# A hybrid backbone step: the RNN branch's gating behind its gates, two temporaries for Strassen's sums, modulation at every fourth product

## The chip, the cores and the metric

One core of one Trainium2 chip runs the whole kernel. The metric is the device time of one execution in microseconds (us); lower is better. The names in the profile: PE is TensorE (matmuls; PEld its weight loads), DVE VectorE, ACT ScalarE, POOL GpSimd, SP the queue that issues the DMAs.

## The reference

A step of two layers over two groups of tokens that share weights (128 context tokens and 1024 latent tokens, 1152 columns in the kernel). Each layer projects the modulated, normalised input into three mixers (a gated bidirectional RNN, latent attention, windowed attention) and their gates, merges them and adds the result to the residual. What the change touches is the RNN branch, whose product with its SiLU gate is formed in the merge, and the projection of the merge logits:

```python
    mod = jax.nn.silu(cond) @ p["w_mod"] + p["b_mod"]
    shift, scale, gate = jnp.split(mod, 3, axis=-1)
    h = rmsnorm(x, p["g_norm"]) * (1 + scale[:, None, :]) + shift[:, None, :]
    parts = jnp.split(h @ p["w_in"], _in_split_points(), axis=-1)
...
    r = jax.nn.sigmoid((jnp.einsum("blnc,ncd->blnd", xb, w_a).reshape(B, L, D_RNN) + b_a).astype(jnp.float32))
    i = jax.nn.sigmoid((jnp.einsum("blnc,ncd->blnd", xb, w_i).reshape(B, L, D_RNN) + b_i).astype(jnp.float32))
    log_a = LRU_C * r * jax.nn.log_sigmoid(lam.astype(jnp.float32))
    a = jnp.exp(log_a)
    u = jnp.sqrt(-jnp.expm1(2.0 * log_a)) * i * x.astype(jnp.float32)
...
    xc = centred_conv(x_rnn, p["conv_w"], p["conv_b"])
    h_f = rglru_scan(xc, h0_f, p["lru_wa"][0], p["lru_ba"][0], p["lru_wi"][0], p["lru_bi"][0], p["lru_lam"][0], False)
    h_b = rglru_scan(xc, h0_b, p["lru_wa"][1], p["lru_ba"][1], p["lru_wi"][1], p["lru_bi"][1], p["lru_lam"][1], True)
...
    m = jax.nn.sigmoid(merge_logits.astype(jnp.float32)).astype(y_rnn.dtype).reshape(B, L, N_BRANCH, D_MODEL)
    u = (m[:, :, 0] * ((y_rnn * jax.nn.silu(g_rnn)) @ p["w_br_rnn"])
```

## The kernel before

Activations lie with features on the partitions and the 1152 tokens along the free axis, cut into three chunks of 384 (CH). Every fp32 matmul is made of three reduced ones, on a high and a low half of each operand: a `split` casts the high half on ACT (L212) and subtracts for the low half on POOL or DVE (L218); the names end in h and l. A weight is loaded into a ring of three raw buffers (`wr`) and then split.

**The RNN stage** of a layer goes over eight feature tiles of 128 (ft 0 to 7). For each, `rnn_units` gives three units. The *x unit* (tile in, feature ft) has three pieces of 24 matmuls; `ev_x` copies each out of PSUM into `xpad` on ACT, and after the third DVE forms the convolution in `xc` (L563, then L566 three times), ACT casts `xh`, POOL subtracts `xl`. The *g unit* (also tile in, feature 8 + ft) has three such pieces; `ev_g` takes a sigmoid into `gsil` on ACT (L577) and multiplies on DVE (L578), which makes the SiLU. The *gates* are 12 pieces of three matmuls on xh and xl (tile g), each evicted by a sigmoid on ACT (L591) into r0, i0, r1 or i1, through three PSUM buffers. After the last gate `scan()` follows: tanh, exp and sqrt on ACT (L604 to L613), eight long elementwise operations and four scan instructions on DVE (L608 to L621), the sum of both directions (L624), two multiplications with gsil (L625, L626) and the store to `yr` (L627). `gsil`, `xc`, `xpad`, `xh` and `xl` are one buffer each.

PE's order is the order of the program (`manual_schedule`). `steps(ft)` takes 18 pieces of a tile, and after piece i as many *fillers* as the table RF has at i: pieces of other projections (tm with 384, 288 or 256 columns, and in), whose PSUM tile is another one; a filler in three is followed by a piece of a mod unit. So 18 pieces are, in order, x (3), g (3) and 12 gates; at tile 0 x and g stand interleaved (`both`). The fillers stand behind the third g piece (3), the fourth and the eighth gate (1 each) and the last gate (2). The evictions of the fillers go through two buffers `eo` (ocq, ock, oqs, okv, osl, osg) and DMAs. On ACT, DVE and POOL a scheduler sets the order by the readiness that it computes; each engine runs its queue strictly in that order.

**The Strassen stage** follows: `combine` forms sums of quadrants of the activations, T1, T2, T4 and a last one that overwrites B12, four elements each, with three DVE operations (L839 to L841), a cast on ACT and a subtraction on DVE. Each element uses one of the five slots of the tile `et` in rotation; slots 0, 1 and 2 are afterwards c1, xs and u2, into which the products are gathered. Then come 11 pairs of seven products (tile st, weights wsh and wsl); `evac` gathers the products (L903 to L918), and after every fifth product `mod_step` takes a piece of a mod unit. Layer 1 has no mod units.

Of the kernel before, what the change touches and what calls it, by code (L numbers as in the profile page):

```python
# [34 lines left out]
V_BMOD, V_G, V_CW, V_CB, V_BA, V_BI, V_LAM, V_H0, V_N = 0, 24, 32, 64, 72, 88, 104, 120, 136  # L35
R_QN, R_KN, R_SINK, R_N = 0, 384, 640, 648

RF = (0,) * 5 + (3, 0, 0, 0, 1, 0, 0, 0, 1, 0, 0, 0, 2)
M_SCORE = set("a0 a1 a2 b1 b2 b0 ra0 ra1 ma xa sa na rb0 rb1 mb xb sb nb c cr cx cs cn".split())
M_START = (  # L40
# [154 lines left out]
def _backbone(ctx, tc, nc, a, depth):  # L195
# [302 lines left out]
    for l in range(depth):  # L498
# [34 lines left out]
        with ExitStack() as rst:  # L533
# [17 lines left out]
            def rnn_units(ft):  # L551
# [21 lines left out]
                def ev_g(c, ps):  # L573
                    if c == 0:
                        r["gsil"] = rp.tile([P, T], F32, tag="gsil", name=f"gsil{l}_{ft}")
                    o = r["gsil"][:, c * CH:(c + 1) * CH]
                    nc.scalar.activation(out=o, in_=ps, func=ACT.Sigmoid)  # L577
                    nc.vector.tensor_tensor(out=o, in0=o, in1=ps, op=ALU.mult)  # L578

                def gate(d, g, c, w):  # L580
                    gh, gl = w
                    xh, xl = r["xh"], r["xl"]
                    if c == 0:
                        t = "ri"[g] + str(d)
                        r[t] = rp.tile([P, RW], F32, tag=t, name=f"{t}{l}_{ft}")
                    dst, vb = r["ri"[g] + str(d)], (V_BA, V_BI)[g]
                    c0, c1 = c * CH, (c + 1) * CH if c < 2 else RW
                    ps = psr.tile([P, 512], F32, tag="a", name=f"g{l}_{ft}_{d}{g}{c}")
                    j = 2 * d + g
                    mm3(ps[:, 0:c1 - c0], [((gh[:, j], gl[:, j]), (xh[:, c0:c1], xl[:, c0:c1]))])  # L590
                    nc.scalar.activation(out=dst[:, c0:c1], in_=ps[:, 0:c1 - c0], func=ACT.Sigmoid,  # L591
                                         bias=sv[:, vb + 8 * d + ft:vb + 8 * d + ft + 1])
                    if g == 1 and c == 2:
                        nc.gpsimd.tensor_tensor(out=dst, in0=dst, in1=r["xc"], op=ALU.mult)
                        if d == 1:
                            scan()

                def scan():
                    rr, ii = [r["r0"], r["r1"]], [r["i0"], r["i1"]]
                    tt = [f(rp.tile([P, RW], F32R, tag=t, name=f"t{t}{l}_{ft}")) for t in ("xh", "xl")]  # L600
                    gsil = r["gsil"]
                    for d in range(2):
                        j = 8 * d + ft
                        nc.scalar.activation(out=tt[d], in_=rr[d], func=ACT.Tanh, scale=L["s4"][:, j:j + 1])  # L604
                    for d in range(2):
                        j = 8 * d + ft
                        nc.scalar.activation(out=rr[d], in_=rr[d], func=ACT.Exp, scale=L["m8"][:, j:j + 1])
                        nc.vector.scalar_tensor_tensor(out=rr[d], in0=rr[d], scalar=1.0, in1=tt[d], op0=ALU.add, op1=ALU.mult)  # L608
                        nc.vector.scalar_tensor_tensor(out=rr[d], in0=rr[d], scalar=-2.0, in1=tt[d], op0=ALU.add, op1=ALU.mult)
                        nc.vector.scalar_tensor_tensor(out=tt[d], in0=rr[d], scalar=2.0, in1=rr[d], op0=ALU.add, op1=ALU.mult)  # L610
                        nc.gpsimd.tensor_scalar(out=rr[d], in0=rr[d], scalar1=1.0, scalar2=1.0, op0=ALU.mult, op1=ALU.add)
                    for d in range(2):
                        nc.scalar.activation(out=tt[d], in_=tt[d], func=ACT.Sqrt, scale=-1.0, bias=tiny_t[:, 0:1])  # L613
                    for d in range(2):
                        nc.vector.tensor_tensor(out=ii[d], in0=ii[d], in1=tt[d], op=ALU.mult)
                        for s0, s1, ctxp in ((0, NL, False), (CTX, CTX + P, True)):
                            av, uv, hv = rr[d][:, s0:s1], ii[d][:, s0:s1], tt[d][:, s0:s1]
                            if d == 1:
                                av, uv, hv = av[:, ::-1], uv[:, ::-1], hv[:, ::-1]
                            init = 0.0 if ctxp else sv[:, V_H0 + 8 * d + ft:V_H0 + 8 * d + ft + 1]  # L620
                            nc.vector.tensor_tensor_scan(out=hv, data0=av, data1=uv, initial=init, op0=ALU.mult, op1=ALU.add)  # L621
                    nc.gpsimd.tensor_copy(out=rg[:, l, 0, ft:ft + 1], in_=tt[0][:, CTX + P - 1:CTX + P])
                    nc.gpsimd.tensor_copy(out=rg[:, l, 1, ft:ft + 1], in_=tt[1][:, CTX:CTX + 1])
                    nc.vector.tensor_tensor(out=tt[0][:, 0:CTX + P], in0=tt[0][:, 0:CTX + P], in1=tt[1][:, 0:CTX + P], op=ALU.add)  # L624
                    nc.vector.tensor_tensor(out=gsil[:, 0:NL], in0=gsil[:, 0:NL], in1=tt[0][:, 0:NL], op=ALU.mult)  # L625
                    nc.vector.tensor_tensor(out=gsil[:, NL:T], in0=gsil[:, NL:T], in1=tt[0][:, CTX:CTX + P], op=ALU.mult)  # L626
                    nc.sync.dma_start(out=yr_d[ft], in_=gsil)  # L627
# [4 lines left out]
                    ins = [both(ins, ((0, 0), (0, 1), (1, 0), (1, 1), (0, 2), (1, 2)))]  # L632
                elif ft == 0:
                    ins = [(lambda: first, both(ins, [(i, c) for c in range(NCH) for i in range(2)])[1])]
                return ins + [
                        (lambda: wload(a["w_lru"][l, ft], 4, P, f"lru{l}_{ft}"), gates)]

            def both(us, order):
                return (lambda: [u[0]() for u in us]), [lambda w, i=i, c=c: us[i][1][c](w[i]) for i, c in order]
# [122 lines left out]
            def mod_step(n=3):  # L762
                count[0] += 1
                if count[0] % n == 0 and G:
                    next(G[0], None)

            def steps(ft):
                for i in range(18):
                    if ft == 0 and i == 4:
                        with tc.high_priority(offset=400):  # L770
                            late_norm()
                    next(R)
                    for _ in range(2 if ft == 0 and i == 5 else RF[i]):
                        filler()
                    yield

# [31 lines left out]
            with tc.manual_schedule(engines={mybir.EngineType.PE}):  # L808
# [25 lines left out]

                def combine(dst, a, b):
                    for k in range(4):
                        t = slot[nt[0] % 5]
                        nt[0] += 1
                        nc.vector.tensor_tensor(out=t, in0=f(a[0][k]), in1=f(b[0][k]), op=ALU.subtract)  # L839
                        nc.vector.tensor_tensor(out=t, in0=t, in1=f(a[1][k]), op=ALU.add)  # L840
                        nc.vector.tensor_tensor(out=t, in0=t, in1=f(b[1][k]), op=ALU.subtract)  # L841
                        split(dst[0][k], dst[1][k], t, "act", "dve")
# [24 lines left out]
                def pair(m):  # L867
# [22 lines left out]
                    def product(i, w):  # L890
                        b = (B11, T1, T2, B21, B12, B22, T4)[i]
                        for c0, c1_ in SP:
# [2 lines left out]
                                for z, (x, y) in enumerate(((0, 0), (0, 1), (1, 0))):  # L895
                                    nc.tensor.matmul(ps, w[x][:, k], b[y][k][:, c0:c1_], start=k == 0 and z == 0, stop=k == 3 and z == 2)  # L896
                            evac(i, ps, slice(c0, c1_))
                        mod_step(5)
                        if i == 6 and m + 2 == PAIRED:
                            ys_load()  # L900

# [1111 lines left out]
```

## Time and profile before

| | us |
|---|---|
| median of 3 runs | 3316.56 (3313.89 to 3320.11) |
| the profiled run | 3312.14 |
| its span | 3310.4 |
| PE busy | 3143.1 (95%) |
| POOL / DVE / ACT busy | 1695.9 / 2114.8 / 1608.7 |
| mean granted clock of PE | 0.978 |

The RNN stage runs from 116 to about 640 us in layer 0 and from 1762 to about 2260 us in layer 1, the Strassen stage directly behind it. The waits of PE are read by what released it: "PE g <- ACT r" is time in which the next gate matmul stood until ACT had evicted an r. A timeline row gives start, duration, engine, line, operation, out<-in, form, and in brackets how long the engine had been idle ahead of it and what released it. The granted clock is 1.00 at 2.4 GHz and 0.50 at 1.2 GHz.

### The profile page before, as it was taken

How to read it: one execution, taken by the hardware profiler on the slowest of the kernel's cores; microseconds unless marked ns; L12 is line 12 of the kernel's file. 1: busy time of each engine (PE TensorE's matmuls, PEld its weight loads, DVE VectorE, ACT ScalarE, POOL GpSimd, SP SyncE). 2: the span in 40 equal slices, each digit the busy share in tenths (PEclk: the TensorE clock that was granted, in tenths of full speed). 3: DMA queues.
4: the chain of work that ended last, by engine and by line, in shares of the span. 5: the costliest groups of instructions: out<-in, count | busy, mean ns of one | idle time of the engine just before them, and what ended most of it. 6: DMA issues, size and time to landing. Idle time of an engine off the chain costs nothing. (4 is left out here: it accounts for less than half of the span.)

```text
span 3310.4 us, 54421 instructions
## 1 busy us (share of the span) xinstructions
PE 3143.1 (95%) x20100; PEld 3006.4 (91%) x20100; DVE 2114.8 (64%) x3777; ACT 1608.7 (49%) x3191; POOL 1695.9 (51%) x1328
## 2 busy tenths in 40 slices
PE   7998989899999999999999999998999999999998
PEld 4998989899999999898989999998999999989998
DVE  5554655854344888977575446577344388898766
ACT  4444545333323777764344454543333277776532
POOL 3755656566622444455475456655553144445643
PEclk9999999999999999999999999999999999999999
DMA  5222122233362001456542221222225400045564
GB/s 211 88 89 83 60 89 93 83 109 124 119 210 95 23 25 45 121 163 208 168 150 74 77 69 47 69 75 90 103 99 191 139 21 27 25 109 150 188 202 133
DMA packets 240330, 351.21 MB, mean 106 GB/s; under 512 B 72512, under 2 KB 183232, under 8 KB 239808
## 3 DMA queue, kind: packets, MB, share of 16 engines
q1 hardware_dynamic: 240064, 347.73, 32.8%
q8 instruction: 159, 2.61, 0.3%
q14 instruction: 107, 0.88, 0.1%
HBM read 248.87 MB, written 98.78 MB: 105 GB/s over the span
## 5 line engine op out<-in xcount | busy, mean ns | idle before, releaser
L242 PE MATMUL in<-hh,wh_in 128*128 128x384 f32 x1248 | 428.1, 343 | 5.9 <-DVE osl L725 3.3
L242 PE MATMUL in<-hh,wl_in 128*128 128x384 f32 x1248 | 427.0, 342 | 6.6 <-POOL wl_in L218 6.6
L242 PE MATMUL in<-hl,wh_in 128*128 128x384 f32 x1248 | 428.2, 343 | 4.1 <-DVE hl L423 4.1
L903 DVE TENSOR_TENSOR et<-st,et 128x320 f32<-128x320 f32 (+1 forms) x352 | 152.1, 454 | 281.9 <-PE st L896 281.1
L1256 POOL TENSOR_SCALAR p<-p,mx 128x1152 f32<-128x1152 f32 x128 | 157.8, 1233 | 201.0 <-DVE mx L1253 125.0
L242 PEld LDWEIGHTS in<-hh,wh_in 128*128 128x128 f32 x1248 | 240.0, 192 | 8.8 <-DVE osl L725 4.8
L242 PEld LDWEIGHTS in<-hl,wh_in 128*128 128x128 f32 x1248 | 239.2, 192 | 8.1 <-DVE hl L423 7.9
L242 PEld LDWEIGHTS in<-hh,wl_in 128*128 128x128 f32 x1248 | 239.4, 192 | 7.6 <-POOL wl_in L218 7.6
L1307 DVE TENSOR_TENSOR pl<-pt,ph 128x512 fp32r<-128x512 f32 (+1 forms) x320 | 201.5, 637 | 28.1 <-ACT ph L1303 25.2
L896 PE MATMUL st<-hh,wsl 128*128 128x320 f32 (+1 forms) x704 | 208.4, 296 | 8.3 <-POOL wsl L218 8.3
L1303 ACT CAST ph<-pt 128x512 fp32r<-128x512 f32 (+1 forms) x320 | 170.8, 552 | 91.2 <-PE pt L1296 86.5
L242 PE MATMUL tm<-twh,hh 128*128 128x256 f32 (+2 forms) x720 | 214.4, 298 | 0.0
L242 PE MATMUL tm<-twl,hh 128*128 128x256 f32 (+2 forms) x720 | 213.7, 297 | 0.0
L242 PE MATMUL tm<-twh,hl 128*128 128x256 f32 (+2 forms) x720 | 213.7, 297 | 0.0
L218 POOL TENSOR_TENSOR wsl<-wr_in,wsh 128x512 fp32r<-128x512 f32 x88 | 147.7, 1678 | 122.5 <-ACT wsh L212 122.5
L896 PE MATMUL st<-hh,wsh 128*128 128x320 f32 (+1 forms) x704 | 208.6, 296 | 1.8 <-ACT osg L732 1.8
L896 PE MATMUL st<-hl,wsh 128*128 128x320 f32 (+1 forms) x704 | 208.0, 295 | 0.0
L1296 PE MATMUL pt<-ident,p 128*128 128x128 f32 x1152 | 171.1, 274 | 10.0 <-DVE kl L1166 4.3
L218 POOL TENSOR_TENSOR wl_in<-wr_in,wh_in 128x1024 fp32r<-128x1024 f32 x50 | 133.6, 2675 | 69.8 <-ACT wh_in L212 69.8
L1296 PEld LDWEIGHTS pt<-ident,p 128*128 128x128 f32 x1152 | 132.7, 140 | 34.6 <-DVE pl L1307 12.1
L1321 PE MATMUL o<-ph,v 128*128 128x256 f32 x576 | 153.1, 292 | 0.0
L1321 PE MATMUL o<-pl,v 128*128 128x256 f32 x576 | 145.9, 280 | 0.0
(498 smaller groups left out, 10619.5 us busy)
## 6 DMA issues: line engine op xcount, KB each, us to landing
wr_in<-in_w_fm SPq DMA_DIRECT2D x96, 512.0 KB, 3.4
sg<-et SPq DMA_DIRECT2D x88, 288.0 KB, 2.1
wr_wm<-in_w_mod SPq DMA_DIRECT2D x32, 512.0 KB, 3.4
wr_wo<-in_w_out SPq DMA_DIRECT2D x32, 512.0 KB, 3.6
yr<-gsil SPq DMA_DIRECT2D x16, 576.0 KB, 2.8
msgrnn<-sg SPq DMA_DIRECT2D x48, 192.0 KB, 2.4
u<-msgrnn SPq DMA_DIRECT2D x48, 192.0 KB, 2.5
qr<-qs SPq DMA_DIRECT2D x36, 256.0 KB, 4.3
```

The source lines that it names most:

```text
L218: eng.tensor_tensor(out=lo, in0=src, in1=f(hi), op=ALU.subtract)
L242: nc.tensor.matmul(ps, x, y, start=n == 0, stop=n == last)
L896: nc.tensor.matmul(ps, w[x][:, k], b[y][k][:, c0:c1_], start=k == 0 and z == 0, stop=k == 3 and z == 2)
L903: add = lambda o, y: nc.vector.tensor_tensor(out=o[:, cs], in0=ps, in1=y[:, cs], op=ALU.add)
L1256: nc.gpsimd.tensor_scalar(out=pts[i], in0=pts[i], scalar1=mxs[i][:, 5:6], scalar2=1.0, op0=ALU.mult, op1=ALU.mult)
L1296: nc.tensor.transpose(ps[:, w:w + P], pts[q][:, k * P:(k + 1) * P], ident)
L1303: nc.scalar.copy(out=r["h", j][:, 0:width(j)], in_=r["t", j][:, 0:width(j)])
L1307: nc.vector.tensor_tensor(out=r["l", j][:, 0:width(j)], in0=r["t", j][:, 0:width(j)], in1=f(r["h", j][:, 0:width(j)]), op=ALU.subtract)
L1321: nc.tensor.matmul(O[:, 0:256], V[k][:, h % 4, :], x[:, 256 * i:256 * i + 256], start=k == 0 and e == 0, stop=k == 8 and e == 1)
```

## The change

Three things are changed, as the diff shows. The new function `gated` holds the two multiplications with gsil and the store.

```diff
-RF = (0,) * 5 + (3, 0, 0, 0, 1, 0, 0, 0, 1, 0, 0, 0, 2)
+RF0 = (0,) * 5 + (3, 0, 0, 0, 1, 0, 0, 0, 1, 0, 0, 0, 2)
+RF = (0, 0, 3, 0, 0, 0, 0, 1, 0, 0, 0, 1, 0, 0, 0, 0, 0, 2)
...
                     nc.vector.tensor_tensor(out=o, in0=o, in1=ps, op=ALU.mult)
+                    if ft and c == 2:
+                        gated()
...
                         if d == 1:
                             scan()
+                            if ft == 0:
+                                gated()
...
-                    gsil = r["gsil"]
+                    r["t"] = tt
...
+
+                def gated():
+                    gsil, tt = r["gsil"], r["t"]
                     nc.vector.tensor_tensor(out=gsil[:, 0:NL], in0=gsil[:, 0:NL], in1=tt[0][:, 0:NL], op=ALU.mult)
                     nc.vector.tensor_tensor(out=gsil[:, NL:T], in0=gsil[:, NL:T], in1=tt[0][:, CTX:CTX + P], op=ALU.mult)
                     nc.sync.dma_start(out=yr_d[ft], in_=gsil)
...
-                return ins + [
-                        (lambda: wload(a["w_lru"][l, ft], 4, P, f"lru{l}_{ft}"), gates)]
+                ins.insert(1, (lambda: wload(a["w_lru"][l, ft], 4, P, f"lru{l}_{ft}"), gates))
+                return ins
...
-                    for _ in range(2 if ft == 0 and i == 5 else RF[i]):
+                    for _ in range((RF if ft else RF0)[i]):
...
-                        t = slot[nt[0] % 5]
+                        t = slot[2 + nt[0] % 2 * 2]
...
-                        mod_step(5)
+                        mod_step(4)
```

For tiles 1 to 7 the order of a tile is now x (3), gates (12), g (3); three fillers stand between x and the gates, one behind the fifth gate piece, one behind the ninth and two behind g. At tile 0 three fillers instead of two stand ahead of the gates. All matmuls stay; a filler that is taken earlier is missing at the end of the stage. `combine` uses slots 2 and 4 in turn.

The order of ACT's instructions from the convolved x of tile 3 to its first gate, before (twh, wh_wm and wh_in are weight casts, ock evictions of tm pieces):

```order
L212 CAST xh_3_2455<-xc_3_2450 128x1156
L577 ACT_TABLE_LOAD
L577 ACTIVATE gsil_3_2490<-in_11_0_2465 128x384
L577 ACTIVATE gsil_3_2490<-in_11_1_2493 128x384
L212 CAST wh_in_4_2661<-wr_in_4_2663 128x1024
L577 ACTIVATE gsil_3_2490<-in_11_2_2520 128x384
L664 ACTIVATE ock_6_2572,ssck_6_2573<-tm_1_6_2547 128x256
...
L212 CAST wh_wm_5_3_2651<-wr_wm_5_3_2653 128x1024
L591 ACTIVATE r_3_2667<-g_3_000_2668,sv_110 128x384
```

And now, from the last copy into xpad; the sigmoids of gsil 3 are no longer there:

```order
L562 COPY xpad_508<-in_3_2_2457 128x128
L672 ACTIVATE ock_7_2518,ssck_7_2519<-tm_1_7_2493 128x256
L686 COPY ock_7_2518<-tm_1_7_2493 128x32
L672 ACTIVATE ock_8_2552,ssck_8_2553<-tm_1_8_2527 128x256
L213 CAST twh_2_2573<-twr_2_0_2575 128x2x256
...
L213 CAST xh_3_2489<-xc_3_2484 128x1156
L213 CAST wh_wm_5_3_2563<-wr_wm_5_3_2565 128x1024
...
L732 ACT_TABLE_LOAD
L732 ACTIVATE osl<-in_21_0_2591 128x384
L213 CAST twh_2_2573<-twr_2_3_2587 128x2x256
L594 ACTIVATE r_3_2626<-g_3_000_2627,sv_110 128x384
```

The cast of xh and the evictions of the fillers have stayed; the first gate's eviction now has a sigmoid of a filler ahead of it, with a table load. Behind the gates of tile 2 stand now gsil 2's sigmoids, with a table load of their own, between exp (L612) and sqrt (L618):

```order
L612 ACT_TABLE_LOAD
L612 ACTIVATE r_2_2138<-r_2_2138,m_115 128x1156
L612 ACTIVATE r_2_2071<-r_2_2071,m_115 128x1156
L578 ACT_TABLE_LOAD
L578 ACTIVATE gsil_2_2261<-in_10_0_2236 128x384
L578 ACTIVATE gsil_2_2261<-in_10_1_2264 128x384
L213 CAST wh_lru_3_2399<-wr_lru_3_2401 128x512
L578 ACTIVATE gsil_2_2261<-in_10_2_2291 128x384
L618 ACT_TABLE_LOAD
L618 ACTIVATE txl_2_2206<-txl_2_2206,consts 128x1156
```

Before, a cast and evictions alone stood between the exponential (L607) and the load for the square root (L613); the two loads are now three.

On DVE the convolution of tile 3 (L563, L566) stood among the scan's last instructions before:

```order
L621 SCALAR_TENSOR_TENSOR txh_2_2259<-r_2_2114,sv_110,i_2_2130 128x1024
L621 SCALAR_TENSOR_TENSOR txh_2_2259<-r_2_2114,i_2_2130 128x128
L563 TENSOR_SCALAR xc_3_2450<-xpad_508,sv_110 128x1156
L566 SCALAR_TENSOR_TENSOR xc_3_2450<-xpad_508,sv_110,xc_3_2450 128x1156
L624 TENSOR_TENSOR txh_2_2259<-txh_2_2259,txl_2_2260 128x1155
L566 SCALAR_TENSOR_TENSOR xc_3_2450<-xpad_508,sv_110,xc_3_2450 128x1156
L625 TENSOR_TENSOR gsil_2_1937<-gsil_2_1937,txh_2_2259 128x1024
L626 TENSOR_TENSOR gsil_2_1937<-gsil_2_1937,txh_2_2259 128x128
L566 SCALAR_TENSOR_TENSOR xc_3_2450<-xpad_508,sv_110,xc_3_2450 128x1156
```

And now:

```order
L629 TENSOR_TENSOR txh_2_2205<-txh_2_2205,txl_2_2206 128x1155
L633 TENSOR_TENSOR gsil_2_2261<-gsil_2_2261,txh_2_2205 128x1024
L634 TENSOR_TENSOR gsil_2_2261<-gsil_2_2261,txh_2_2205 128x128
L564 TENSOR_SCALAR xc_3_2484<-xpad_508,sv_110 128x1156
L567 SCALAR_TENSOR_TENSOR xc_3_2484<-xpad_508,sv_110,xc_3_2484 128x1156 x2
```

The convolution now stands behind the gated product of the tile before.

## Rows read from the trace of the kernel before

**Rows 1.** the page's part 1, PE: busy time, share, instructions.

```profile
PE 3143.1 (95%) x20100; PEld 3006.4 (91%) x20100; DVE 2114.8 (64%) x3777; ACT 1608.7 (49%) x3191; POOL 1695.9 (51%) x1328
```

**Rows 2.** the waits of PE: engine, line, waited for: us in total, times, longest.

```profile
PE g L242 <- ACT r L591: 34.9, 8, 6.5
PE st L896 <- POOL wsl L218: 8.3, 1, 8.3
PE mod L311 <- POOL wl_wm L218: 7.8, 3, 5.2
PE g L242 <- ACT xh L212: 6.9, 3, 4.7
PE g L242 <- POOL xl L218: 6.8, 4, 2.3
PE st L896 <- ACT et L905: 5.0, 1, 5.0
```

**Rows 3.** a window: us, busy of PE, PEld, DVE, ACT, POOL, then PEclk.

```profile
315.00:321.80 6.80, 5.47 (x17) 5.47 (x18) 0.25 (x1) 3.58 (x8) 4.68 (x4) 0.50 0.65 181
```

**Rows 4.** the timeline, ACT and PE ahead of tile 3's gates, layer 0.

```profile
304.13 1.28 ACT L577 ACT_TABLE_LOAD   x1 [0.27 <-DMA yr<-gsil]
...
309.77 0.34 PE L242 MATMUL g<-xh,wh_lru 128*128 128x384 f32 x1
...
310.83 0.34 PE L242 MATMUL g<-xh,wh_lru 128*128 128x388 f32 x1
...
311.16 0.19 ACT L678 COPY ock<-tm 128x32 f32<-128x32 f32 x1 [3.17 <-DVE ock L667]
...
315.70 0.58 ACT L591 ACTIVATE r<-g,sv 128x384 f32<-128x384 f32 x1
...
316.33 0.69 PE L242 MATMUL g<-xh,wh_lru 128*128 128x384 f32 x1 [4.81 <-ACT r L591]
```

**Rows 5.** the timeline, DVE between the gates of tiles 4 and 5, layer 0.

```profile
390.85 0.61 DVE L695 TENSOR_TENSOR oqs<-tm,rope 128x64 f32<-128x64 f32 x4
...
394.00 2.10 DVE L608 SCALAR_TENSOR_TENSOR r<-r,txl 128x1156 f32<-128x1156 f32 x1 [2.53 <-ACT r L607]
...
421.01 1.42 DVE L566 SCALAR_TENSOR_TENSOR xc<-xpad,sv,xc 128x1156 f32<-128x1156 f32 x1
...
425.77 1.48 DVE L578 TENSOR_TENSOR gsil<-gsil,in 128x384 f32<-128x384 f32 x3 [3.35 <-ACT gsil L577]
```

**Rows 6.** the timeline, PE and POOL from tile 0's and tile 4's last gates on.

```profile
135.81 0.34 PE L242 MATMUL tm<-twl,hh 128*128 128x384 f32 x1
...
173.77 2.69 POOL L218 TENSOR_TENSOR xl<-xc,xh 128x1156 fp32r<-128x1156 f32 x1 [9.17 <-ACT xh L212]
...
387.41 0.28 PE L242 MATMUL tm<-twh,hh 128*128 128x256 f32 x1
...
418.03 0.28 PE L242 MATMUL tm<-twh,hh 128*128 128x256 f32 x1
...
420.86 0.39 PE L310 MATMUL mod<-wh_wm,sc 128*4 128x512 f32 x1
...
421.78 0.34 PE L242 MATMUL in<-hh,wh_in 128*128 128x384 f32 x1
...
423.77 2.69 POOL L218 TENSOR_TENSOR xl<-xc,xh 128x1156 fp32r<-128x1156 f32 x1 [6.75 <-ACT xh L212]
...
430.26 0.34 PE L242 MATMUL g<-xh,wh_lru 128*128 128x384 f32 x1
```

**Rows 7.** the timeline, ACT, the table load ahead of an exponential.

```profile
139.64 1.28 ACT L607 ACT_TABLE_LOAD   x1
140.93 2.41 ACT L607 ACTIVATE r<-r,m 128x1156 f32<-128x1156 f32 x2
```

**Rows 8.** the timeline, DVE and POOL at the start of the Strassen stages.

```profile
669.24 6.42 DVE L218 TENSOR_TENSOR hl<-et,hh 128x576 fp32r<-128x576 f32 x3
2259.44 22.18 POOL L218 TENSOR_TENSOR wsl<-wr_in,wsh 128x512 fp32r<-128x512 f32 x1 [7.38 <-ACT wsh L212]
```

## The prediction

> **What bounds the kernel now.** I read the page first: TensorE (PE) is busy 3143.1 of 3310.4 us [rows 1], so a change that neither adds nor removes matmuls can only act on the time in which PE stands still, and on its clock. Then the table of PE's waits [rows 2]: the largest item by far is the gate matmuls (tile g) waiting for ScalarE (ACT) to evict an earlier gate (r, L591): 34.9 us in 8 waits, the longest 6.5. The same matmuls wait 6.9 us for xh and 6.8 us for xl, the two halves of the convolved x. Behind the RNN stage the first Strassen products (st) wait 8.3 us for POOL's wsl and 5.0 us for ACT's et, and a mod product 5.2 us for POOL. Third, the clock around one such wait: granted 0.50 from 315.0 to 321.8 us [rows 3], that is 1.2 instead of 2.4 GHz, right after PE had stood 4.81 us [rows 4]. What would take 3.4 us at full clock takes 6.8 there, so such a wait costs its own length and 3.4 us more. Six of the eight waits are long (4.2 to 6.5 us), and I give each such a stretch.
>
> Fourth, why ACT is late, in the stretch before the gates of feature tile 3 [rows 4]. gsil is one buffer. ACT's first instruction of the next gsil, the table load at 304.13, is released by the store of the one before (its idle time ends with the DMA yr<-gsil). ACT runs in order, so the evictions of filler pieces behind it back up: one copy at 311.16 is held 3.17 us for ock on VectorE (DVE). The first gate eviction starts at 315.70; PE has issued three gate pieces into its three accumulators and resumes at 316.33.
>
> **The change, part by part. 1, g behind the gates.** For tiles 1 to 7 ACT's sigmoid into gsil now comes a whole tile after the store of the one before, so the wait on the store goes, and with it the reason for the 34.9 us. I count all of it as gone, and six half-clock stretches: -34.9 - 6 x 3.4 = -55.3. The lower bound of this gain is 0 (a rival below).
>
> What is late next? The x pieces. Take tile 4 to 5 [rows 5, 6]. The last gate of tile 4 ends near E = 387.4, where the fillers begin. DVE starts on the scan at 394.00 (ACT's exp released it), and the convolution, queued among the scan's instructions, ends at 421.01 + 1.42 = 422.4, E + 35. Then ACT's cast to xh and POOL's xl, which ends at 423.77 + 2.69 = 426.5, E + 39. PE came to the next gates at 430.26: 3.8 us of cover. At tile 0 the same reading gives xl's end at 173.77 + 2.69 = 176.5, E + 40.7, with E = 135.8. The tiles between lie a few us around these two. The window, PE's work from E to the next gates, is counted in the new order with the prices of rows 6: an in or g piece 4.24 (two in 430.26 - 421.78), a 256-column tm piece 2.83, a mod 0.92; a 384-column tm piece is taken as 4.2, having the columns of an in piece. Tile 0 to 1: it loses the three g pieces and one filler is moved ahead of it: 5 tm, 3 in, 1 mod = 34.9 (48.5 before). Tile 3 to 4: 3 g + 3 x + 5 tm = 39.8; tile 5 to 6 some 40. The other four tiles: 42.5 to 45.8. (Layer 1 is 0 to 2.3 shorter, having no mods.)
>
> DVE's queue ahead of the end of the convolution grows: three gsil multiplies, 0.5 each (1.48 for three), in all tiles 1 to 6, and at tiles 3 and 5 three rope evictions of about 1.0 each that stood behind it [rows 5]. So I put xl's end at E + 40.5 at tile 0 (no multiply added), 41 to 43 at 1, 2, 4, 6, and 44 to 44.5 at 3 and 5 (40 + 1.5 + 3). New waits of g for xl: 40.5 - 34.9 = 5.6 at tile 0, 44.4 - 39.8 = 4.6 at tile 3, 44.2 - 40.1 = 4.1 at tile 5: 14.3 a layer, 28.6 in both, and 6 x 3.4 = 20.4 of clock: **+49**. The other eight windows stand within 2 us of their bound, on either side; I take 0.6 us and a part of a clock stretch, 0.9, for each: +12 (bounds 0 and 51, a rival).
>
> At the first tile, the filler moved ahead of the gates (4.2 us) covers most of the waits for xh and xl that rows 2 show; the longest is 4.7: -4 a layer, and in one of the two layers the clock stretch goes with it: **-11**. A wait at tile 6 for the same two goes into the new ones: -3.
>
> The sigmoids of gsil now stand between exp and sqrt, so the order holds 16 more table loads, and at tiles 1, 4, 6 the sigmoid's load falls on the first gate eviction. A load takes 1.28 us and the next activation starts 0.01 us after it [rows 7]. PE issues two further gate pieces meanwhile, 310.83 - 309.77 = 1.06 us, and an eviction takes 0.58 [rows 4]: 1.28 + 0.58 - 1.06 = 0.8, six times: **+5**. Bounds: 0 and 6 x 1.28 = 7.7. The Trainium skill, "ScalarE: Activation LUTs", section "What ACT_TABLE_LOAD costs", speaks against this part: it has a further drain of about 1.38 us beside a load of the same 1.28. By that the six would cost 13 instead of 5, and the time would be 8 us higher, still on the same side. The trace agrees on the load, and shows no drain in this place: 139.64 + 1.28 = 140.92, and the exponential starts at 140.93.
>
> **2, the work behind the last gates.** Three g pieces, 12.7 us, come behind the gates of tile 7, and one filler of 2.8 goes ahead of them in exchange: 9.9 us more PE work there, in each layer, and as much less before. Layer 1: PE waited 8.3 us for wsl, since one subtraction on POOL took 22.18 us beside DVE's combine [rows 8]. That wait ends when the combine ends, counted from tile 7's gates, so 9.9 us more work covers it, and about 1 us comes on top from the three gsil multiplies: -9. Layer 0: a product waited 5.0 us for the eviction of the first (ACT et) and the mod 5.2 for POOL [rows 2]; the eviction stood behind the last hl of the combine, 6.42 us for three [rows 8], and the same sum gives -8.5. **-17.5**.
>
> **3, two temporaries.** A difference of the combine now waits for the cast and the subtraction of the one two before, not five before. In the new order two or more instructions of the other element stand between an element's last step and its lo, at 2.1 us each where hl ran (6.42 / 3), and that covers a cast on ACT. Taken at 0, hidden by the second element; its price, if ACT is held elsewhere, is a rival. The gain, that the first products' c1 need not wait for a slot, is in the layer 0 term.
>
> **4, mods.** The same number of mod pieces; those in the Strassen products come one in four, so they finish two pairs earlier. Two loads through the ring close to each other cost PE about 1.3 us in rows 2 ((7.8 - 5.2) / 2): I take **+3** (0 to 10).
>
> The sum: -55.3 + 49 + 12 - 11 - 3 + 5 - 17.5 + 3 = -17.8. The profiled run took 3312.14 for a span of 3310.4, and stands 0.13% under the median 3316.56. From the median: 3298.
>
> **The rivals.** *The chain fits* (the new waits at tiles 3 and 5 don't come, because DVE's scan meets less of POOL and runs at its short durations): without (4.6 + 4.1) x 2 + 4 x 3.4 = 31 us, 3267. For it: before, tile 4's xl ended at E + 39 and not later [rows 6]. Against: nothing in the change takes work from DVE or POOL.
>
> *The convolution chain becomes the bound everywhere* (slower). x now ends three pieces later, with only three fillers (8.6 to 13.7 us) between it and the gates, and it needs about 10 us (convolution 5.1, cast 1.2, xl 2.7, gaps). It decides from xl's end later than E + 45 at tiles 1, 2, 4, 6: then 8 more windows wait 3.0 + 3.4 us, 51 in place of 12: 3337. For it: the margin is 2 us, and the convolution stands behind the gated product in the new queue. Against: the two readings of before, E + 39 and E + 40.7 [rows 6].
>
> *The combine pauses* with two temporaries: 10 us a layer (0 to 20), at 16 elements with a wait of 0.6 each: 3318, no change.
>
> *The gate evictions stay late*: the evictions through two eo buffers [rows 4] back up without the store, too. With half of term 1 left: 3298 + 28 = 3326.
>
> **How the numbers follow.** Chances: the forecast 0.47 (own range 3284 to 3312), the chain fits 0.16, the chain bounds 0.16, the combine pauses 0.13, evictions stay late 0.08. Faster by over 0.2% (6.6 us, about what a measurement of this kernel can tell from no change): 0.42 + 0.16 = 0.58. Within 0.2%: 0.05 of the forecast, 0.11 of the combine, 0.01: 0.17. Slower: 0.16 + 0.02 + 0.07 = 0.25. The range 3265 to 3333 leaves out the far half of the chain rivals.
>
> **What would show it.** Right: in the waits, "g <- ACT r" under 8 us and "g <- xl" over 25, at tiles 0, 3, 5 of both layers; "st <- POOL wsl" gone; clock stretches at half where g waits for xl. Wrong: g waiting for xl at tiles 1, 2, 4, 6 too (the chain bounds); no wait for xl (it fits); DVE waiting for ACT in the combine; ACT r still over 20 us.

## The result, and the profile after

The changed kernel is slower: 3341.24 us (3335.12 to 3344.41) against 3317.18 beside it, a ratio of 1.0071 with an interval of 1.0053 to 1.0088. The forecast was 3298, with a range of 3265 to 3333. The first two lines of the page of the changed kernel, to be read against rows 1:

```profile
span 3338.6 us, 54386 instructions
PE 3156.4 (95%) x20100; PEld 3015.7 (90%) x20100; DVE 2130.3 (64%) x3777; ACT 1634.2 (49%) x3207; POOL 1652.5 (49%) x1328
```

The 20100 matmuls are the same and PE is busy for 13.3 us longer, with a mean granted clock of 0.975 instead of 0.978: more of them ran at half clock. The span grew by 28.2, so the other 15 us are time in which PE stood. Its waits (columns as in rows 2: us in total, times, longest; names as before, line numbers moved by the diff):

```profile
PE g L243 <- POOL xl L219: 36.3, 15, 3.6
...
PE g L243 <- ACT xh L213: 35.1, 11, 7.0
...
PE mod L312 <- POOL wl_wm L219: 7.2, 4, 2.3
...
PE g L243 <- ACT r L594: 3.7, 4, 1.2
...
PE mod L311 <- ACT wh_wm L213: 3.2, 2, 1.6
...
PE g L243 <- ACT i L594: 2.5, 2, 1.3
```

The waits for ACT's r fell from 34.9 to 3.7 us, as forecast, and POOL's wsl and ACT's et have left the table. In their place the gates wait 36.3 us for xl and 35.1 for xh, 71.4 where rows 2 have 13.7, and the two kinds of mod waits add up to 10.4 where rows 2 have 7.8 (5.2 of those from the start of the Strassen stage). Where the time went, from the starts and ends of the gates (g) and products (st) in the two traces; the third product is the third in order:

| stretch, us | before | after |
|---|---|---|
| layer 0, start to first gate | 115.9 | 119.1 |
| first gate to end of the last | 458.7 | 460.4 |
| from there to the third product | 101.5 | 104.0 |
| from there to the end of the last product | 250.5 | 261.0 |
| layer 1, first gate to end of the last | 436.9 | 448.2 |
| from there to the third product | 89.6 | 88.5 |
| from there to the end of the last product | 234.5 | 234.5 |

By the prices of rows 6, PE has 14.1 us less work than before in each of the two gates' stretches (three g pieces behind them, 12.7, a filler of 4.2 ahead of them, one of 2.8 pulled in) and 9.9 more in the two starts of the Strassen stage. So the gates' stretches lost 15.8 and 25.4 us against their work, the starts of the Strassen stages gained 7.4 and 11.0, and the products of layer 0, whose work is the same, lost 10.5.

A window between gates, tile 1 to 2 of layer 0. Timeline rows of four engines; the last gate of tile 1 ended at E = 197.4:

```profile
231.03 0.29 PE L243 MATMUL tm<-twh,hh 128*128 128x288 f32 x1
...
232.32 0.27 ACT L562 COPY xpad<-in 128x128 f32<-128x128 f32 x1
...
232.63 2.63 DVE L564 TENSOR_SCALAR xc<-xpad,sv 128x1156 f32<-128x1156 f32 x1 [3.52 <-ACT xpad L562]
...
238.49 1.41 DVE L567 SCALAR_TENSOR_TENSOR xc<-xpad,sv,xc 128x1156 f32<-128x1156 f32 x1
...
239.99 1.16 ACT L213 CAST xh<-xc 128x1156 fp32r<-128x1156 f32 x1 [0.82 <-POOL ssck L673]
...
241.22 2.64 POOL L219 TENSOR_TENSOR xl<-xc,xh 128x1156 fp32r<-128x1156 f32 x1 [0.65 <-ACT xh L213]
...
243.91 0.44 PE L243 MATMUL g<-xl,wh_lru 128*128 128x384 f32 x1 [2.02 <-POOL xl L219]
```

PE finishes the third x piece where the first filler starts, at 231.03, E + 33.6. The convolution starts at 232.63; DVE had been idle for 3.52 us and waited for the copy into xpad. It ends at 239.90, xl at 243.86. PE had three fillers and a mod piece to do behind x, came to the gates at 241.56 and stood 2.02 us for xl. From x to xl it is 12.8 us, and the cover is 10.5. Tile 4 to 5 is the worst window (E = 382.6):

```profile
422.82 2.00 ACT L213 CAST wh_in<-wr_in 128x1024 fp32r<-128x1024 f32 x2 [7.67 <-DMA wr_in<-in_w_fm]
...
424.72 0.36 ACT L561 COPY xpad<-in 128x256 f32<-128x256 f32 x1
...
425.28 1.69 DVE L564 TENSOR_SCALAR xc<-xpad,sv 128x1156 f32<-128x1156 f32 x1 [6.29 <-ACT xpad L562]
...
434.97 0.69 PE L243 MATMUL g<-xh,wh_lru 128*128 128x384 f32 x1 [6.99 <-ACT xh L213]
```

ACT has casts of the fillers' weights ahead of the last x copy in its queue, and the DMA for them was late: 7.67 us of idle time. So the convolution started 6.29 us after DVE was free, and PE stood 6.99 us. The clock behind that wait, to be read against rows 3:

```profile
435.00:441.80 6.80, 4.77 (x14) 4.37 (x15) 1.02 (x2) 3.54 (x7) 4.95 (x2) 0.50 0.28 80
```

### The profile page after: what moved, and what is told of

It reads as the page before. It is cut to its first block, busy times and chain, and to the rows that moved or that the text cites. A ratio compares the mean times of both kernels' runs of the same rounds, so it can differ in the third digit from the quotient of the medians.

```text
span 3338.6 us, 54386 instructions
## 1 busy us (share of the span) xinstructions
PE 3156.4 (95%) x20100; PEld 3015.7 (90%) x20100; DVE 2130.3 (64%) x3777; ACT 1634.2 (49%) x3207; POOL 1652.5 (49%) x1328
## 5 line engine op out<-in xcount | busy, mean ns | idle before, releaser
L219 POOL TENSOR_TENSOR wl_in<-wr_in,wh_in 128x1024 fp32r<-128x1024 f32 x50 | 126.2, 2528 | 116.7 <-ACT wh_in L213 116.5
L219 POOL TENSOR_TENSOR wsl<-wr_in,wsh 128x512 fp32r<-128x512 f32 x88 | 114.9, 1307 | 135.7 <-ACT wsh L213 135.6
```

The costliest lines, as they stand in the source:

```text
L219: eng.tensor_tensor(out=lo, in0=src, in1=f(hi), op=ALU.subtract)
```

## The experiments

Times are medians, ratios go against the kernel before on the same chip. Each diff is against the kernel named.

**The mods' place: e1_mod5** (against the changed kernel).

```diff
-                        mod_step(4)
+                        mod_step(5)
```

> The changed kernel with the mod pieces at every fifth product again; the rest of the change stays. In the traces the Strassen stage of layer 0, from its third product to its last, took 261.0 us against 250.5 before, with five waits for a mod weight (1.65, 2.26, 0.97, 1.59, 2.30 us) that before has one of. Theory 'two mod loads meet in the ring': about -10 us, 3331, and the stage back at 250 to 252. Rival 'the stage is longer because of the combine's late end or the products' slots': within 2 us of 3341.

3324.73 us, ratio 1.0029 (1.0020 to 1.0039): 16.5 us off the changed kernel, more than expected. The products of layer 0 take 248.6 us again. The changed kernel's DMA queue and PE at the place (an SPq row shows issues; x2 are two in a row):

```profile
700.76 5.10 SPq L226 DMA_DIRECT2D wr_wm<-in_w_mod  x2
...
705.20 0.39 PE L311 MATMUL mod<-wh_wm,sc 128*4 128x512 f32 x1 [1.65 <-ACT wh_wm L213]
...
707.85 0.40 PE L312 MATMUL mod<-wl_wm,sc 128*4 128x512 f32 x1 [2.26 <-POOL wl_wm L219]
```

Two mod loads in a row go through the ring of three buffers between two pairs of weights. The first was issued at 700.76, behind 1.8 us of waiting for POOL's sx, and PE came to its product at 703.55, 2.8 us later: PE stands for its cast and then for POOL's half of it. Two loads in a row are not enough for that. The changed kernel has a third such pair at 730.44, whose first load is 6 us ahead of PE, and there the wait is 0.97 us, as at the one pair that e1_mod5 has (0.96 at 823.62). The same stretch of products in the changed kernel and in e1_mod5 (window, busy of PE, PEld, DVE, ACT, POOL, clock, DMA share, GB/s):

```profile
760.00:830.00 70.00, 66.11 (x471) 63.21 (x470) 27.06 (x55) 23.79 (x39) 39.87 (x29) 0.95 0.34 115
```

```profile
760.00:830.00 70.00, 69.04 (x514) 67.13 (x513) 26.37 (x56) 25.03 (x42) 43.90 (x31) 1.00 0.36 120
```

In 70 us the mean clock is 0.95 against 1.00, besides the waits. The late first load comes twice (700.76 and 802.57). Three pairs of runs differ in the mods' place alone: 16.5 here, 11.1 (e3_gfront against e9_slots, below) and 14.1 us (e4_fill5 against e8_fill5_mod5); by their ratios, each to before on its own chip, 13.9, 11.9 and 15.6.

**The slots: e2_slot5** (against the changed kernel) and **e9_slots** (the same line the other way, alone in the kernel before).

```diff
-                        t = slot[2 + nt[0] % 2 * 2]
+                        t = slot[nt[0] % 5]
```

> The changed kernel with the combine over five slots again. Theory 'two temporaries cost nothing, and give little': within 4 us of 3341, the stretch from the last gate to the third product within 4 us of 104 (layer 0) and 88.5 (layer 1). Rival 'the combine pauses with two': 10 to 20 us faster, 3321 to 3331.

> The kernel before with two temporaries in the combine and nothing else. Theory 'the two temporaries remove the wait of the first products for the combine (8.3 us in layer 1, 5.0 in layer 0, with their half clock)': 12 to 18 us faster, 3297 to 3303. Rival 'the gain of the run with parts two and three came from elsewhere': within 4 us of 3315.

e2_slot5: 3340.43, ratio 1.0077 (1.0055 to 1.0098): nothing. e9_slots: 3299.99, ratio 0.9951 (0.9932 to 0.9971): 16 us faster, by this line alone. From the last gate to the third product it takes 94.2 and 80.6 us (101.5 and 89.6 before). DVE and POOL of e9_slots at the start of layer 1's Strassen stage, against rows 8:

```profile
2252.15 2.53 DVE L839 TENSOR_TENSOR et<-hh,sth_r 128x576 f32<-128x576 f32 x2
...
2252.41 1.65 POOL L218 TENSOR_TENSOR wsl<-wr_in,wsh 128x512 fp32r<-128x512 f32 x1 [8.78 <-ACT wsh L212]
...
2254.60 1.42 DVE L840 TENSOR_TENSOR et<-et,hl 128x576 f32<-128x576 f32 x2
```

POOL's subtraction takes 1.65 us and not 22.18: with two temporaries DVE takes each step for two elements in a row, and a POOL instruction gets in at such a pair, which then takes 2.53 instead of 1.42. Why it gets in here and not in rows 8 the traces don't show. In e2_slot5 one of POOL's subtractions still takes 13.21 us (at 2296.96), and PE doesn't wait for it, since it has g's work behind the gates. So the wait for wsl can go in two ways, by other work that covers it (the changed kernel with either kind of slots) or by the two temporaries. Each gives about the same, and both together give it once.

**Parts two and three alone: e3_gfront** (the changed kernel with g ahead of the gates and the old table).

```diff
-                ins.insert(1, (lambda: wload(a["w_lru"][l, ft], 4, P, f"lru{l}_{ft}"), gates))
-                return ins
+                return ins + [(lambda: wload(a["w_lru"][l, ft], 4, P, f"lru{l}_{ft}"), gates)]
...
```

> The changed kernel with g ahead of the gates and the old table of fillers: parts two (two temporaries) and three (mods at every fourth product) alone. Theory 'the loss lies in the RNN stage, where x ends too late for its convolution': the waits of g for xh and xl (71 us in the changed kernel) go back to about 14, those for ACT's r come back (35), and the time is before's plus the mods' 10: 3325 to 3330. Rival 'parts two and three are the whole loss': 3341.

3311.08, ratio 0.9987 (0.9977 to 0.9996): 14 to 19 us under what was expected, because the temporaries' gain (e9_slots) was not in the expectation. The waits for xh and xl are back at 13.7, those for r at 35.6:

```profile
PE g L243 <- ACT r L592: 35.6, 8, 7.2
...
PE g L243 <- ACT xh L213: 6.9, 3, 4.6
PE g L243 <- POOL xl L219: 6.8, 4, 2.3
```

Moving g with three fillers behind x thus costs 28 to 30 us on top of the other two parts.

**The cover behind x: e4_fill5, e8_fill5_mod5, e16_fill4_mod5, e17_fill6_mod5** (against the changed kernel; the last three with mod_step(5) too). Four: 4 behind x and 1 behind g. Six: 6 behind x and 1 in the gates.

```diff
-RF = (0, 0, 3, 0, 0, 0, 0, 1, 0, 0, 0, 1, 0, 0, 0, 0, 0, 2)
+RF = (0, 0, 5, 0, 0, 0, 0, 1, 0, 0, 0, 1, 0, 0, 0, 0, 0, 0)
```

> The changed kernel with five fillers between x and the gates and none behind g (three and two before): x ends two fillers (6 to 8 us) sooner, the number of pieces in each window stays. Theory 'x ends too late': the convolution starts 1 to 4 us sooner, up to the end of the gated product, and each of 14 windows loses 1 to 3 us of waiting with some of its half clock: -25 to -45 us, 3296 to 3316. Rival 'the convolution is late because it stands behind the gated product and runs slowly beside POOL': -10 to 0 us, 3331 to 3341.

> Five fillers between x and the gates, none behind g, and mods at every fifth product. If both effects add: 3305 - 13 = 3292 (3288 to 3297). If the mods' place only costs where the Strassen stage starts late: 3300 to 3306.

> The changed kernel with mods at every fifth product and four fillers between x and the gates (one behind g). Three gave 3324.7, five 3291.2. Theory 'the cover behind x decides, a filler at a time': the waits of g for xh and xl lie between 71 and 11 us, 3302 to 3314. Rival 'it is the two fillers behind g that hold x back or something of their order': at either end, 3320 or more, or 3294 or less.

> The same with six fillers between x and the gates, one among the gates and none behind g. Theory 'with five, the convolution already starts when DVE has done the gated product, so more cover gives only what xl still waits (11 us), and the gates lose a filler that hides their evictions': 3285 to 3300, waits of g for xh and xl under 5, for ACT's r or i over 24. Rival 'more cover goes on paying': under 3282.

| fillers behind x | mods at | us | ratio (interval) | g waits for xh + xl | for r |
|---|---|---|---|---|---|
| 3 (changed) | 4 | 3341.24 | 1.0071 (1.0053 to 1.0088) | 71.4 | 3.7 |
| 5 | 4 | 3305.31 | 0.9970 (0.9960 to 0.9981) | 11.3 | 23.7 |
| 3 (e1_mod5) | 5 | 3324.73 | 1.0029 (1.0020 to 1.0039) | 71.2 | 3.5 |
| 4 | 5 | 3291.59 | 0.9928 (0.9912 to 0.9945) | 25.6 | 13.9 |
| 5 | 5 | 3291.23 | 0.9923 (0.9902 to 0.9945) | 11.1 | 24.2 |
| 6 | 5 | 3285.67 | 0.9903 (0.9888 to 0.9917) | 2.3 | 22.6 |

PE's waits in e4_fill5, e16_fill4_mod5 and e17_fill6_mod5, in this order:

```profile
PE g L243 <- ACT r L594: 23.7, 9, 5.5
...
PE g L243 <- POOL xl L219: 11.3, 5, 2.7
```

```profile
PE g L243 <- POOL xl L219: 22.3, 10, 3.3
...
PE g L243 <- ACT r L594: 13.9, 6, 6.9
```

```profile
PE g L243 <- ACT r L594: 22.6, 12, 4.1
...
PE g L243 <- POOL xl L219: 2.3, 1, 2.3
```

One filler behind x decides 33 us. As PE waits less for xl, waits for ACT's r come back: the gates are reached earlier, and ACT has not caught up. From four to five the waits for xh and xl fall by 14.5 us and those for r grow by 10.3; what takes the rest of the gain is not shown. The expected fall, a filler at a time, did not come: with four fillers the waits lie between the two ends, as the theory has it, but the time (3291.59, not 3302 to 3314) is where the rival put it, at the end of five. With six the expectation held (3285 to 3300), but for the waits for r, 22.6 and not over 24.

With six fillers behind x and the old place of the mods, the kernel is also 14 us under e9_slots (0.9903 against 0.9951, the intervals are apart). So moving g, with the fillers where they stand in that run, is worth something once x is covered, but far from the 55.3 us that the forecast gave it.

**g one tile late: e7_glate** (against the changed kernel): x of a tile, then g of the tile before, then the gates; mods at every fifth product; the sum of both directions goes to the buffer of i0, so that xh is free. At tile 1, which has no g ahead of its gates, six fillers stand there.

```diff
...
-                R = stream([u for ft in range(8) for u in rnn_units(ft)])
+                U = [rnn_units(ft) for ft in range(8)]
+                R = stream(U[0] + U[1][0:2] + [u for ft in range(2, 8) for u in (U[ft][0], U[ft - 1][2], U[ft][1])] + [U[7][2]])
...
```

> The changed kernel with mods at every fifth product and another order: x of a tile first, then g of the tile before, then the gates (g one tile late), the fillers where they stood before the change; the sum of both directions goes to another buffer. Theory 'the gain of taking g off its buffer's store is real, and was lost only because x came three pieces later': both the waits for ACT's r and those for xh and xl stay small (under 20 us together with their first tiles), 3265 to 3285. Rival 'the gate evictions are late for other reasons too, and the convolution is late because of DVE's queue': waits of 40 us or more, 3295 to 3325.

3307.12, ratio 0.9971 (0.9961 to 0.9981). The first half of the rival held, and the time with it; its second half, a convolution that is late for DVE's queue, did not, since the waits for xh and xl are gone (2.3 us). The sigmoids of gsil (L579) wait for PE alone in this trace, neither for a store nor for DVE's product, and r is waited for as long as ever; the row below is ACT ahead of a gate that is late by 5.46 us:

```profile
PE g L244 <- ACT r L595: 35.6, 11, 5.7
...
500.50 0.62 ACT L214 CAST twh<-twr 128x512 fp32r<-128x512 f32 x1 [7.62 <-DMA twr<-in_w_tm]
```

ACT stands 7.62 us for a weight of a filler. This run puts the prediction's first term in doubt, and the next four go to the kernel before.

**What holds ACT back: e10_prod_i0, e11_ckfirst, e13_ock3, e15_three** (against the kernel before; the first takes gsil's store away, the second moves a copy, the third adds a buffer, e15_three is all three).

```diff
-                    nc.vector.tensor_tensor(out=gsil[:, 0:NL], in0=gsil[:, 0:NL], in1=tt[0][:, 0:NL], op=ALU.mult)
+                    nc.vector.tensor_tensor(out=ii[0][:, 0:NL], in0=gsil[:, 0:NL], in1=tt[0][:, 0:NL], op=ALU.mult)
...
-                    nc.sync.dma_start(out=yr_d[ft], in_=gsil)
+                    nc.sync.dma_start(out=yr_d[ft], in_=ii[0][:, 0:T])
```

```diff
-                rms_row(ps[:, 0:256], 256, R_KN, o[:, 0:256], f"ck{l}_{t}")
                 nc.scalar.copy(out=o[:, 256:288], in_=ps[:, 256:288])
+                rms_row(ps[:, 0:256], 256, R_KN, o[:, 0:256], f"ck{l}_{t}")
```

```diff
-                o = ep.tile([P, 384], F32, tag="eo", name=f"ock{l}_{t}")
+                o = ep.tile([P, 288], F32, tag="ek", bufs=1, name=f"ock{l}_{t}") if t in (1, 4, 8) else ep.tile([P, 384], F32, tag="eo", name=f"ock{l}_{t}")
...
-                tmp = ep.tile([P, 256], F32, tag="rt", name=f"rt{nm}")
+                tmp = ep.tile([P, 256], F32, tag="rt", bufs=1, name=f"rt{nm}")
```

> The kernel before with one edit: the product of the SiLU gate and the scan goes to the buffer of i0 and is stored from there, so that the next sigmoid into gsil waits for DVE's product and no longer for the store (landing 2.8 us after its issue). Theory of the prediction (the store is the reason for the 34.9 us of waiting for ACT's r): these waits fall by 3 us at each of six places, with a part of the half clock, -18 to -38 us, 3278 to 3298. Rival (ACT is late at the gates because it waits for filler evictions and weight loads in its queue, and the store is made up for anyway): within 6 us of 3316, the waits for r stay over 28 us.

> The kernel before with one edit: of an ock eviction, ACT's copy of the last 32 columns comes ahead of the normalisation and not behind it, so that ACT no longer waits for POOL's and DVE's part of the eviction. Theory 'ACT's queue backs up behind the evictions at tiles 2 and 3': the four waits for r at 252, 316, 1894 and 1956 us (20.0 us) fall by half or more, with their half clock: -12 to -30 us, 3286 to 3304. Rival 'the store of gsil or the weight loads set when ACT comes to the gates': within 5 us of 3316.

> The kernel before with a third eviction buffer for three of the nine ock pieces (the second, fifth and ninth; the rope's scratch is single instead of double to make room). Nothing else. Theory 'ACT comes late to the gates of tiles 2 and 3 because the third filler eviction in a row waits for one of two buffers to be stored': the waits for r at 252, 316, 1894 and 1956 us (20.0 us in all) fall under 6, with their half clock: -15 to -34 us, 3282 to 3301; the waits at 438 and 2075 us, which lie behind weight loads, stay. Rival 'ACT is late for the sigmoids of gsil or the weights there too': within 5 us of 3316.

> The kernel before with the three edits at once that alone moved 0 to 3 us: product to the buffer of i0, ock's copy first, a third eviction buffer for three ock pieces. Theory 'ACT's lateness at the gates of tiles 2 and 3 is a chain of several near-equal links, and each alone is covered by the next': the waits for r at tiles 2 and 3 (20.0 us before) fall under 8, -12 to -28 us, 3288 to 3303. Rival 'something else sets when ACT comes to the gates': the waits stay over 14, 3308 to 3316.

e10_prod_i0: 3312.85, ratio 0.9995 (0.9985 to 1.0005), no change. Its wait for r, and ACT ahead of the gates of tile 5:

```profile
PE g L242 <- ACT r L591: 35.6, 8, 6.8
...
420.10 1.28 ACT L577 ACT_TABLE_LOAD   x1 [14.40 <-DVE i L626]
...
430.20 0.62 ACT L212 CAST twh<-twr 128x512 fp32r<-128x512 f32 x1 [4.25 <-DMA twr<-in_w_tm]
...
434.62 1.04 ACT L212 CAST wh_in<-wr_in 128x1024 fp32r<-128x1024 f32 x1 [2.29 <-DMA wr_in<-in_w_fm]
```

The table load of the sigmoid is released by DVE's product and no longer by the DMA (rows 4 have the DMA there). It changes nothing: ACT then waits for two weight loads, 4.25 and 2.29 us. The wait for the product itself (14.40 us of idle time) stays in this run; in e7_glate it is gone too, and r is waited for all the same. e11_ckfirst: 3315.29, ratio 0.9998 (0.9989 to 1.0007), no change. Two rows of ACT ahead of the gates of tiles 2 and 3:

```profile
250.50 0.18 ACT L677 COPY ock<-tm 128x32 f32<-128x32 f32 x1 [7.12 <-DMA gm<-osl]
...
312.51 0.19 ACT L677 COPY ock<-tm 128x32 f32<-128x32 f32 x1 [4.55 <-DMA ck<-ock]
```

The wait for DVE (3.17 us in rows 4) is gone, and ACT waits for an eviction buffer to be stored instead. e13_ock3: 3311.57, ratio 0.9986 (0.9976 to 0.9996). The wait for r and the row of ACT at tile 3:

```profile
PE g L242 <- ACT r L591: 32.2, 8, 7.8
...
306.79 0.19 ACT L678 COPY ock<-tm 128x32 f32<-128x32 f32 x1 [3.19 <-DVE ock L667]
```

With the third buffer the waits at tile 2 fall from 4.9 and 4.2 to 2.0 and 1.2 us, and at tile 3 ACT waits for DVE's part of ock again. e15_three: 3294.70, ratio 0.9934 (0.9919 to 0.9949):

```profile
PE g L242 <- ACT r L591: 22.7, 6, 7.5
```

The three edits gave 3.1, 0.7 and 3.4 us one by one (against their own runs of before), and 21.9 together. The waits for r at tile 2 vanish; 3.7 and 2.9 us are left at tile 3, and those at tile 5 (6.1 and 7.5), which stand behind weight loads in e10_prod_i0's rows, stay, as they were left alone. So the 20.0 us at tiles 2 and 3 had several links, each nearly as late as the next. No run has two of the three edits, so which of them are needed stays open, and no run takes the weight loads at tile 5 away.

**Toward a better kernel: e12_fill5_mod5_ck, e14_fill5_mod5_ock3, e19_fill6_ock, e18_three_slots.** The first three put the edits on ock (copy first; a third buffer for every third piece; both) on five, five and six fillers. e18_three_slots is e15_three with the two temporaries: g is not moved and the mods stay at every fifth product.

> Five fillers between x and the gates, mods at every fifth product, and the copy of the last 32 columns of ock ahead of its normalisation. If the waits for r that are left at tiles 2 and 3 (5.5, 5.4, 2.8, 0.8 us and clock stretches) come from that chain of evictions: 3291 - 15 = 3276 (3268 to 3284). If they don't: 3288 to 3294.

> Five fillers between x and the gates, mods at every fifth product, and the third eviction buffer for every third ock. The waits for r that are left at tiles 2 and 3 of both layers (5.5, 5.4, 2.8, 0.8 us) fall by half or more if the two buffers are their cause: 3291 - 10 to - 20 = 3271 to 3281. If not: 3288 to 3294.

> The changed kernel with six fillers behind x, mods at every fifth product, ock's copy first and a third eviction buffer for every third ock. If the waits for r that are left (22.6 us in 12) are the evictions of ock at tiles 2 and 3 as in the kernel before: 3285.7 - 5 to - 15 = 3271 to 3281. If they are spread over other causes: 3283 to 3290.

> The kernel before with g ahead of the gates as it was, the three edits on ACT's queue and two temporaries in the combine. If the two act in stages that don't touch (gates; start of the Strassen stage), they add: 3294.7 - 15 = 3280 (3276 to 3284). If the combine's start had been shortened already: 3290 or more.

e12_fill5_mod5_ck: 3290.33, ratio 0.9924 (0.9906 to 0.9942); e14_fill5_mod5_ock3: 3297.78, ratio 0.9952 (0.9938 to 0.9967); e19_fill6_ock: 3286.54, ratio 0.9906 (0.9882 to 0.9929). None gains, and the second is 6.5 us above its run without the edit, with intervals that just overlap; the reason stays open. The waits for r are 23.9, 21.2 and 19.7 us, where they were 24.2, 24.2 and 22.6: with g behind the gates the links on ock hold at most 3 us of them. e18_three_slots: **3280.39 us, ratio 0.9891 (0.9872 to 0.9911)**, the lowest median of all, though its interval overlaps that of e17_fill6_mod5, and the sum of its parts (3294.7 less 16 is 3279). Its page:

```profile
span 3281.3 us, 54389 instructions
PE 3132.6 (95%) x20100; PEld 2996.3 (91%) x20100; DVE 2124.0 (65%) x3777; ACT 1607.3 (49%) x3191; POOL 1668.5 (51%) x1328
```

PE is busy 10.5 us less than in rows 1, with the same matmuls and a mean granted clock of 0.984 instead of 0.978: fewer ran at half clock.

## Why the prediction was wrong

**The step that failed is the end of xl in the windows, and with it the term +49 +12.** The prediction put it at E + 41 to 43 for tiles 1, 2, 4, 6 and 44 to 44.5 for 3 and 5. In layer 0 the trace has 46.5, 45.3, 55.1 and 49.1, and 47.4 and 47.0; tile 0, forecast 40.5, has 41.4. The forecast followed the chain from the scan's start through DVE's queue, as it was in the kernel before, where x was long done. With g of the tile before ahead of x, the convolution starts on x's last copy into xpad (at tiles 1 to 5 of layer 0 within 0.3 us of its end). That start was there to be had: three g and three x pieces and two fillers put x at E + 32 to 34, and with the 10 us that the rival counted behind x, xl ends at 42 to 44 at best. The convolution took 7.3 us at tile 1, not 5.1, beside POOL and with an eviction among its parts, and at tile 4 the copy itself was late. The runs with four to six fillers show that this is the cause: the cover alone brought the waits for xh and xl from 71 to 2 us. The rival "the convolution chain becomes the bound everywhere" had the mechanism and nearly the time (3337); it was given 0.16, because its margin was read off the old chain.

**Mods: +3 forecast, 11 to 16.5 measured.** The cost of one meeting of loads was known from one row of 1 us. What was missed is that at one in four a load is issued only 2.8 us ahead of its product, twice, with 3.9 us of waiting each time and a clock that falls behind it.

**The waits for r: right in number, wrong in reason.** They went (34.9 to 3.7), mostly since PE came later, not because ACT came sooner. In e10_prod_i0, which takes only the store away, they stay at 35.6, and in the runs with five and six fillers 22.6 to 24.2 us of them return, so at most some 12 went with the move itself, with this much cover. That the forecast number came true is luck. The row on which it rested, a table load with 0.27 us of idle time ended by the DMA, shows that the store held ACT for 0.27 us there; what ACT did in the 11 us between it and the gate was read, but the next links were not priced. The rival "the gate evictions stay late" (0.08) had this right.

**What held.** The start of the Strassen stages: forecast -17.5, measured -7.4 - 11.0 = -18.4, by the cover as foreseen. That the two temporaries give nothing beside it held too (e2_slot5); that they give 16 us alone was not foreseen. The first tile: layer 0's waits for xh and xl are gone, layer 1's 6.7 us are 2.2. The table loads: +5 forecast; the waits for r and i together are 6.2 us, and no run takes the loads away.

**The clock.** It is at half around the long waits, as forecast, but the price of a stretch was read too high. In rows 3 the clock is at half from 315.00 on, while PE stood until 316.33, so PE worked in 5.47 of the 6.8 us: that costs 2.7 us and not 3.4 (2.4 in the changed kernel's window, with 4.77). As the forecast counts stretches on both sides of its sum, this moves it little; but the changed kernel has more of them. The granted clock falls to 0.50 at 12 of its 16 sets of gates (eight tiles, two layers), and at 9 before.

The sum missed by 42 us (-18 forecast, +24 measured). Waits for xl and xh are some 36 us longer than the forecast has them, and the mods 8 to 13.5 dearer. That leaves little for the rest, but waits and clock overlap, so the parts are not exact. (The forecast's own sum, 17.8 off 3316.56, gives 3298.8; it was rounded down.)

## What to carry to other kernels

When a piece of work is moved ahead of another on the busy engine, the chain that hangs on the second one starts later: follow it from its new start, and count what is left behind it as cover, before looking at the queues it went through in the old order. A wait that names one releaser may be the last of several near-equal ones; taking one away can show next to nothing until the others are gone too (3.1, 0.7 and 3.4 us here, and 21.9 together). And the idle time in the row says how much that one releaser held. Two edits that remove the same wait don't add, and the cheaper one is found by trying each alone.

## What the runs showed of the hardware

A POOL subtraction of 128x512 took 22.18 us beside a run of some thirty DVE instructions of two inputs without a gap (the kernel before), and 1.65 us in e9_slots, where the DVE pair beside it took 2.53 instead of 1.42. The Trainium skill, "SBUF — State Buffer", section "SBUF: two separate sides", has DVE and GpSimd share a pair of ports as an exclusive lock, in which the loser blocks for the whole instruction. The traces agree that one of the two stands still; they show besides that POOL can stand through a whole run of DVE instructions. It need not: some 10 us ahead of the long one, three POOL instructions of the kernel before got through in 1.78, 1.69 and 2.92 us (from 2245.63 on), and DVE's beside them took up to 2.90. What decides this is not shown.

Between the slowest and the fastest kernel here PE's busy time differs by 24 us with the same matmuls (3156.4 and 3132.6, mean granted clock 0.975 and 0.984). The spans differ by 57.3 us, so 33.5 are time in which PE stood: by this estimate an us of standing cost some 0.7 us more in the clock.
